# Two planes for the experts' rows and a fourth column sum held back, in a two-block fp32 kernel

## The chip, the cores and the metric

The kernel runs on one core of one Trainium2 chip. The metric is the device time of one execution in microseconds (us), the median of several runs; lower is better. The profile describes one execution, which has a time of its own.

## The reference, cut to what matters

T = 1024 tokens of width D = 1024 in fp32 pass through two blocks. The first has gated linear attention, pooling and a mixture of experts; the second a gated convolution and a dilated window attention.

```
h = rmsnorm(x, g1);  proj = h @ w_in          # q, k, v, r, a_low, u_pool, gates
log_a = log_sigmoid(a_low @ w_alpha_up + b) / 16
x = x + merged(gla, pool, gates) @ w_out
h2 = rmsnorm(x, g2)
# each token: the best of 4 groups, in it the 2 best of 8 experts (32 experts in all)
out[token] += gate * ((silu(h2 @ w_gate[e]) * (h2 @ w_up[e])) @ w_down[e])   # 2 rows a token
x = rmsnorm(x + out, gf)
# second block
proj2 = rmsnorm(x, norm_w) @ w_in_2           # conv part, q, k, v, z
for (window, dilation) in ((128,1), (512,4), (2048,16)):   # each of 8 heads
    banded softmax attention, with its log-sum-exp
y_attn = mix of the three by softmax of the log-sum-exps
x = x + concat(y_conv, y_attn * silu(z)) @ w_out_2
```

## The kernel before

All large products run in "split" fp32: an operand is written as a high part and a low part (ACT casts the high one, DVE subtracts the low one, both at L127), and `mm3` issues three matmuls (L161 to L163). A **column sum** (`cols_first`, L165) is 8 such triples, 24 matmuls of 512 columns, into one PSUM bank; `low_rank` (L177) is the like for the 16 low-rank columns of `a_low`. A framework inserts the waits: a tile is taken from a pool by tag, and an allocation waits until an older tile of that tag is free. The tag "blk" has 26 buffers of 4 KB a partition and serves almost every large tile; "wr" has 4 for raw weights, "vt" 3 for attention values. Order on each engine is program order. The program itself shifts steps: `late.at(n, fn)` runs `fn` n calls of `late.step()` later, and each column sum makes two such calls.

**Block 1** runs in two halves of 512 tokens (`half(0)`, `half(1)`). In half 0 the row scales of the first norm (1/rms) aren't ready when the first sums are. The low-rank sum and the sums of q0 and q1 are therefore held in PSUM without scales (`OWE = 3`). Then `h.owe` (L232) spreads the scales over partitions by 8 matmuls (L236) of the scales against an identity, and `take` (L245) multiplies the held sums while it copies them out. The steps are due at `2*OWE`, `2*OWE - 2 - 2*j` after their sums.

**Routing**: `route_rows(t)` takes each block of 128 tokens when its block-1 result x1 is finished. It writes x1 to `x_acc` in DRAM, turns it over on TensorE, computes logits, writes the scaled row h2 to `h2_d`. For the last block t = 7, h2 is made ahead of the logits by two POOL products (L531, L532). `slots` and `row_tables` produce, for each expert, the token numbers (`row_idx`) and weights (`row_wgt`) of up to 96 rows.

**Experts**: for each of 32 experts, POOL gathers 96 rows by an indirect DMA (L980), TensorE turns them, runs gate, up and down products with weights that SP loads in blocks of 512 KB, ACT scales the rows, and POOL adds them to `x_acc` by an indirect DMA that accumulates (`add_rows`, L985):

```
G.indirect_dma_start(out=x_acc, out_offset=..row_idx.., in_=src[:n], ..., compute_op=OP.add)
```

The rows of expert 31 stay on the chip and are added with selecting matmuls (`add_last`, L1068 to L1076). A loop for overflowing experts (L1128) runs zero times here. After it, `load_cols(x_acc, "x2c")` (L308) loads the first 512 tokens as four tiles of 256 columns; these loads wait for all the adds.

**Block 2** begins on those four tiles (second norm, turn, convolution products), then loads tokens 512 to 1023 (`load_x2`, L1219), then q, k, v. **Attention** is a stream of 48 items: 4 pairs of heads by 3 dilations by 4 parts. Per item: `load_values` (vt, SP), `powers` (scores at L1500, bias and minimum on DVE at L1506, exponential on ACT at L1508), `turn_powers` (transposes at L1526, copies at L1528 and L1530), `weigh` (L1559). The stream starts `powers` two items ahead of `weigh`. `by_class` (L1487) copies q and k into dilated order, on POOL, twice a pair of heads. `spread` (L1607) loads the mixing weights (zb), and `close_heads` (L1617) applies them. Between items stand pieces of the output product.

Of the kernel before, what the change touches and what calls it, by code (L numbers as in the profile page):

```python
# [20 lines left out]
P = 128  # L21
# [44 lines left out]
def first_then_second_block(ctx: ExitStack, tc: tile.TileContext, a: dict, out: bass.AP):  # L66
# [12 lines left out]
    OWE = 3  # L79
# [400 lines left out]
    row_idx = C.tile([P, NE], I32, name="row_idx")  # L480
    row_wgt = C.tile([P, NE], F32, name="row_wgt")
# [38 lines left out]
    last_h2 = []  # L520

    def route_rows(t, x1):
# [17 lines left out]
        def turn():  # L540
            for q in range(2):
                ps = psum((P, 4, P))
                for i in range(4):
                    PE.transpose(ps[:, i, :], xv[:, 4 * q + i, :], ident)
                split(hi[:, 4 * q:4 * q + 4, :], lo[:, 4 * q:4 * q + 4, :], ps)
            late.at(D2 if t < 4 else D5, logits)

# [12 lines left out]
        def folded(lt):  # L560
# [5 lines left out]
            if t < NT - 1:  # L566
                h2 = blk("h2", (P, D))
                V.scalar_tensor_tensor(h2, x1, r, g2, op0=OP.mult, op1=OP.mult)
                G.dma_start(h2_d[t * P:(t + 1) * P], h2)

# [17 lines left out]
    def route_half(hf):  # L588
# [26 lines left out]
        val = blk("val", (P, 4, 2, 5, NE), BF16)  # L615
        A.activation(val[:, :, :, 0, :], oh[:, ts], AF.Copy, scale=pcol)
        for i in range(4):
            A.activation(val[:, i, :, 1, :], oh[:, 4 * hf + i], AF.Copy, scale=float(4 * hf + i + 1))
        late.at(1 if hf else PLACES, lambda: places(hf, val, gp, e1, e2))

    def places(hf, val, gp, e1, e2):
# [31 lines left out]
        V.tensor_mul(val.rearrange("p t k v e -> p (t k) v e")[:, :, 2:, :],  # L653
# [4 lines left out]
    def slots(hf, val, sels):  # L658
        if hf == 0:
            slot_ps.append(psum((P, 5, NE)))  # L660
# [7 lines left out]
    def row_tables(idx, w, ps, n, pool):  # L668
        f = pool.tile([P, n], F32, name="ri_f", tag=f"rif{n}", bufs=1)
        e = pool.tile([P, n], F32, name="ri_e", tag=f"rie{n}", bufs=1)  # L670
        sv = pool.tile([P, 5, n], F32, name="ri_s", tag=f"ris{n}", bufs=1)
# [3 lines left out]
        V.scalar_tensor_tensor(idx, f, -float(P), e, op0=OP.add, op1=OP.add)  # L675
        V.tensor_add(e, sv[:, 2, :], sv[:, 3, :])
# [3 lines left out]
    def half(hf):  # L680
# [30 lines left out]
        else:  # L711
            w_q += pair(w_in, 0)
        if hf == 0:
# [21 lines left out]
        for j, w in enumerate(w_q):  # L735
            def emit_q(ps, j=j):
                if h.rb is None and hf == 0:
                    late.at(2 * OWE - 2 - 2 * j, lambda: h.take(qT[:, j, :], ps, 0.125))
                else:
                    h.take(qT[:, j, :], ps, 0.125)  # L740

            cols_first(w, h, emit_q)
        for j, w in enumerate(pair(w_in, 256)):
            cols_first(w, h, lambda ps: h.take(kT[:, j, :], ps))
# [223 lines left out]
    SY.dma_start(h2_d[(NT - 1) * P:], last_h2[0])  # L968
    load_expert(3)
    late.flush()  # L970
    row_tables(row_idx, row_wgt, slot_ps[0], NE, R)
# [63 lines left out]
    def down(e):  # L1035
# [10 lines left out]
        if e < NE - 1:  # L1046
            add_rows(yt, row_idx[:, e:e + 1], CAP)
# [9 lines left out]
    last_idx = S.tile([P, 1], I32, name="last_idx", bufs=1)  # L1057
    picks = blk("picks", (P, 512), F32R)

    def place_last():  # L1060
        at = S.tile([P, 5], F32, name="last_at", bufs=1)
        V.tensor_copy(last_idx, row_idx[:, NE - 1:NE])
        V.tensor_copy(at[:, 4:], last_idx)
        for i in range(4):
            V.tensor_scalar(at[:, i:i + 1], at[:, 4:], float(-P * i), None, op0=OP.add)
            V.tensor_scalar(picks[:, i * P:(i + 1) * P], iota_s, at[:, i:i + 1], None, op0=OP.is_equal)

    def add_last(c):  # L1068
        for j in range(2):
            ps = psum((P, 2, 256))  # L1070
            for i in range(2):
                b = 2 * j + i
                for part in range(2):
                    PE.matmul(ps[:, i, :], picks[:CAP, b * P:(b + 1) * P], last_y[1 + part][:CAP, 256 * c:256 * c + 256],
# [51 lines left out]

    end_reg = nc.values_load(n_more[0:1, 0:1], min_val=0, max_val=NOB)
    with tc.For_i(0, end_reg, 1):  # L1128
# [24 lines left out]
        rv = E.tile([P, NT, 2, 5], BF16, name="rv")  # L1153
# [5 lines left out]
        sp = psum((P, 5))  # L1159
# [7 lines left out]
        row_tables(li, lw, sp.rearrange("p (a b) -> p a b", b=1), 1, E)  # L1167
# [36 lines left out]
        add_rows(lyt, li, P)  # L1204
# [10 lines left out]
    def load_x2():  # L1215
        xs = []
        for t in range(4, NT):
            xt = blk(f"x2_{t}", (P, D))
            SY.dma_start(xt, x_acc[t * P:(t + 1) * P])  # L1219
            xs.append(xt)  # L1220
# [52 lines left out]
    yc = [blk("yc0", (P, T))] + [W.tile([P, T], F32, name=f"yc{j}") for j in range(1, 4)]  # L1273
# [3 lines left out]
    qT = [blk(f"qT{j}", (P, T)) for j in range(4)]  # L1277
    for j in range(4):
        V.memset(qT[j][:, 0:1], 0.0)
        V.memset(kT[j][:, 0:1], 0.0)  # L1280
# [5 lines left out]
    def conv(hf, cc):  # L1286
# [35 lines left out]
        def convolve(m):  # L1322
            ct, u = 2 * cc + m, us[m]
            cv = yc[ct]
# [85 lines left out]
    for f in c0[:4] + c1[:4] + c0[4:] + c1[4:] + attn_gate(0):  # L1410
        f()
    x2 = load_x2()
# [167 lines left out]
    def mix_weights(hp):  # L1580
# [16 lines left out]
        def spread():  # L1597
            ps = psum((48, P))
            PE.transpose(ps, sw.rearrange("p c h b -> p (c h b)"), ident)
            swT = W.tile([48, P], F32, name="swT", tag="swT", bufs=1)  # L1600
# [84 lines left out]
    for g in range(-2, NS):  # L1685
        if g + 2 < NS:
            hp, cfg, pr = stream[g + 2]
            if g == -2:
# [89 lines left out]
```

## Time and profile before

| | |
|---|---|
| median of 3 runs | 1626.17 us (1624.89 to 1628.64) |
| the profiled execution, its own time | 1627.21 us |
| its span | 1625.5 us |
| mean granted TensorE clock | 0.972 |
| DMA, mean over the span | 167 GB/s, 272.01 MB |

PE is TensorE's matmuls, DVE VectorE, ACT ScalarE, POOL GpSimd, SP the engine that issues most loads. The span runs from the first to the last instruction of the profiled execution; its time is a little longer. A granted clock of 1.00 is the full level, 0.50 half of it.

### The profile page before, as it was taken

Reading aid. Unit: us, or ns where it says so; the run is one execution under the profiler, and the core shown is the slowest. Engines: PE = TensorE matmul, PEld = TensorE weight load, DVE = VectorE, ACT = ScalarE, POOL = GpSimd, SP = SyncE. Lnnn points to the kernel's source line nnn. Section 1 sums busy time; section 2 is a strip of 40 time slices with the busy share of each in tenths; the row PEclk is TensorE's granted clock in tenths of the full one; section 3 lists DMA queues with packets and bytes.
Section 4 is the critical chain, followed back from the end, with each engine's and each line's share of the span. In section 5 each row is a group of like instructions: output and inputs, shape, how many; then the busy total and the mean of one; then the engine's idle time right before and its main releaser. Section 6 shows DMA issues by size and latency. Waiting matters only on the chain. (4 is left out here: it accounts for less than half of the span.)

```text
span 1625.5 us, 24026 instructions
## 1 busy us (share of the span) xinstructions
PE 1535.9 (94%) x8678; PEld 1266.6 (78%) x8678; DVE 1021.1 (63%) x2278; ACT 801.2 (49%) x1635; POOL 210.8 (13%) x196
## 2 busy tenths in 40 slices
PE   7999999999999994999989897999999999999899
PEld 6888888887888874998888786888877787666667
DVE  5596444667644355998877686766655545676663
ACT  4434323453433232888777684524443326866550
POOL 1000000000000003232232111200000100243311
PEclk9999999999999996999999998999999999999999
DMA  6233334436323458999999996434423331445445
GB/s 193 65 82 106 103 109 163 136 115 195 104 80 115 142 215 281 295 270 319 328 312 335 296 335 194 156 102 164 149 88 104 104 103 41 120 119 147 103 137 169
DMA packets 168022, 272.01 MB, mean 167 GB/s; under 512 B 32689, under 2 KB 111932, under 8 KB 167773
## 3 DMA queue, kind: packets, MB, share of 16 engines
q1 hardware_dynamic: 154204, 232.13, 44.5%
q0 software_dynamic: 13680, 38.32, 8.5%
q8 instruction: 69, 1.13, 0.3%
q14 instruction: 53, 0.43, 0.1%
q10 hardware_dynamic: 16, 0.00, 0.0%
HBM read 243.92 MB, written 39.59 MB: 174 GB/s over the span
## 5 line engine op out<-in xcount | busy, mean ns | idle before, releaser
L127 ACT CAST wh<-wr 128x512 fp32r<-128x512 f32 (+1 forms) x248 | 170.6, 716 | 341.9 <-PE ps L162 192.5
L127 DVE TENSOR_TENSOR wl<-wr,wh 128x512 fp32r<-128x512 f32 (+1 forms) x248 | 202.3, 832 | 169.4 <-ACT wh L127 162.7
L127 DVE TENSOR_TENSOR wl<-ew,wh 128x1024 fp32r<-128x1024 f32 x144 | 172.6, 1220 | 44.3 <-ACT wh L127 43.6
L161 PE MATMUL ps<-h,wh 128*128 128x512 f32 x448 | 176.8, 395 | 0.0
L127 ACT CAST wh<-ew 128x1024 fp32r<-128x1024 f32 x144 | 149.7, 1052 | 54.4 <-PE ps L163 34.8
L163 PE MATMUL ps<-h,wl 128*128 128x512 f32 x448 | 175.3, 391 | 0.0
L162 PE MATMUL ps<-h,wh 128*128 128x512 f32 x448 | 175.3, 391 | 0.0
L161 PE MATMUL ps<-g,wh 128*128 128x512 f32 x320 | 126.1, 395 | 0.0
L162 PE MATMUL ps<-g,wh 128*128 128x512 f32 x320 | 125.2, 392 | 0.0
L163 PE MATMUL ps<-g,wl 128*128 128x512 f32 x320 | 124.8, 391 | 0.0
L161 PE MATMUL ps<-wh,xh 128*96 128x256 f32 x384 | 112.3, 293 | 6.2 <-ACT act L1023 6.2
L162 PE MATMUL ps<-wl,xh 128*96 128x256 f32 x384 | 110.9, 289 | 1.5 <-DVE wl L127 1.5
L163 PE MATMUL ps<-wh,xh 128*96 128x256 f32 x384 | 110.8, 289 | 0.0
L163 PEld LDWEIGHTS ps<-h,wl 128*128 128x128 f32 x448 | 84.6, 189 | 17.8
L161 PEld LDWEIGHTS ps<-h,wh 128*128 128x128 f32 x448 | 84.7, 189 | 17.5
L162 PEld LDWEIGHTS ps<-h,wh 128*128 128x128 f32 x448 | 84.6, 189 | 17.2
L985 POOL DMA_INDIRECT x_acc<-yt,row_idx x31 | 52.1, 1679 | 208.2 <-ACT yt L1045 147.6
L161 PE MATMUL ps<-wh,g 128*128 128x512 f32 x192 | 76.3, 398 | 0.0
L528 POOL DMA_DIRECT2D x_acc<-x x7 | 3.8, 536 | 551.7 <-DVE x L930 294.0
L163 PE MATMUL ps<-wh,g 128*128 128x512 f32 x192 | 75.1, 391 | 0.0
L162 PE MATMUL ps<-wl,g 128*128 128x512 f32 x192 | 74.9, 390 | 0.0
L161 PEld LDWEIGHTS ps<-wh,xh 128*96 128x96 f32 x384 | 65.8, 171 | 8.2 <-ACT act L1023 7.0
(455 smaller groups left out, 3642.0 us busy)
## 6 DMA issues: line engine op xcount, KB each, us to landing
wr<-in_w_in_dram SPq DMA_DIRECT2D x128, 512.0 KB, 3.9
ew<-in_w_exp_down_dram SPq DMA_DIRECT2D x64, 512.0 KB, 9.7
ew<-in_w_exp_gate_dram SPq DMA_DIRECT2D x64, 512.0 KB, 8.0
ew<-in_w_exp_up_dram SPq DMA_DIRECT2D x64, 512.0 KB, 9.5
wr<-in_w_out_dram SPq DMA_DIRECT2D x24, 512.0 KB, 3.9
xs<-xb_rows POOLq DMA_DIRECT2D x28, 256.0 KB, 3.3
x<-in_x_dram SPq DMA_DIRECT2D x12, 512.0 KB, 6.3
zb<-sw_d SPq DMA_DIRECT2D x24, 256.0 KB, 5.2
```

Of the source, the lines that this page charges most:

```text
L127: both = A.copy(hi, src), V.tensor_sub(lo, src, hi.bitcast(F32))
L161: PE.matmul(ps, lhs[0], rhs[0], start=start, stop=False)
L162: PE.matmul(ps, lhs[0], rhs[1], start=False, stop=False)
L163: PE.matmul(ps, lhs[1], rhs[0], start=False, stop=stop)
L528: G.dma_start(x_acc[t * P:(t + 1) * P], x1)
L985: G.indirect_dma_start(out=x_acc, out_offset=bass.IndirectOffsetOnAxis(ap=idx[:n], axis=0), in_=src[:n], in_offset=None, bounds_check=T - ...
```

## The change

Five edits stand in one diff.

1. `OWE` 3 to 4: the column sum of k0 is also held without scales, so `h.owe` comes after it.
2. Experts' rows are written to rows of their own, in two planes of a DRAM array `y_d` of 2T rows (plane k for a token's k-th expert, `put_rows`), instead of added to `x_acc`. For that the slot product has a sixth column (k), `row_tables` makes `row_place`; 8 writes of 512 KB zeros clear rows 0 to 511 of both planes during half 1. The x2c loads are moved ahead of the overflow loop; after it 8 loads "y2c" bring the two planes, and `add_last` adds them (2 more DVE operations for each of 4 tiles). `load_x2` has 8 more loads and 8 more additions.
3. In `route_rows` the POOL products of the last block are gone: the block before waits with its h2 until the last block has been turned, and the last block's h2 is made on DVE after its logits; its write goes through POOL's queue in place of SP's.
4. `picks`, `yc[0]` and `qT` are allocated later.
5. Attention: `LEAD` 3 instead of 2, 4 "vt" buffers instead of 3, the copies of `by_class` on DVE, `swT` in tag "tmp".

```diff
-    OWE = 3
+    OWE = 4
...
+    y_d = tc.dram_tile([2 * T, D], F32, name="y_rows")
...
-        else:
-            h2 = blk("h2", (P, D))
-            G.tensor_mul(h2, x1, r.to_broadcast([P, D]))
-            G.tensor_mul(h2, h2, g2)
-            G.dma_start(x_acc[t * P:(t + 1) * P], x1)
-            last_h2.append(h2)
...
+            while unscaled:
+                unscaled.pop()()
...
+            if t == NT - 2 and NT - 1 not in turned:
+                unscaled.append(scaled_rows)
+            else:
+                scaled_rows()
...
-        val = blk("val", (P, 4, 2, 5, NE), BF16)
+        val = blk("val", (P, 4, 2, 6, NE), BF16)
...
+        for k in range(2):
+            A.activation(val[:, :, k, 5, :], oh[:, ts, k, :], AF.Copy, scale=float(k))
...
+        V.scalar_tensor_tensor(f, sv[:, 5, :], float(T), f, op0=OP.mult, op1=OP.add)
+        V.scalar_tensor_tensor(place, f, -float(P), e, op0=OP.add, op1=OP.add)
...
+        if hf == 1:
+            zero = blk("zero", (P, D))
+            G.memset(zero, 0.0)
+            for i in range(8):
+                r0_ = T * (i // 4) + P * (i % 4)
+                late.at(2 * i, lambda r0_=r0_: SY.dma_start(y_d[r0_:r0_ + P], zero))
...
-    def add_rows(src, idx, n):
-        G.indirect_dma_start(out=x_acc, out_offset=bass.IndirectOffsetOnAxis(ap=idx[:n], axis=0),
-                             in_=src[:n], in_offset=None, bounds_check=T - 1, oob_is_err=False, compute_op=OP.add)
+    def put_rows(src, place, n):
+        G.indirect_dma_start(out=y_d, out_offset=bass.IndirectOffsetOnAxis(ap=place[:n], axis=0),
+                             in_=src[:n], in_offset=None, bounds_check=2 * T - 1, oob_is_err=False)
...
     def add_last(c):
+        for y in yc2[c]:
+            V.tensor_add(xc2[c], xc2[c], y)
...
+    xc2, turn_part2 = load_cols(x_acc, "x2c")
     end_reg = nc.values_load(n_more[0:1, 0:1], min_val=0, max_val=NOB)
     with tc.For_i(0, end_reg, 1):
...
-    xc2, turn_part2 = load_cols(x_acc, "x2c")
-    add_rows(last_y[0], last_idx, CAP)
+    yc2 = []
+    for c in range(4):
+        yc2.append([])
+        for k in range(2):
+            yt = blk("y2c", (P, 4, 256))
+            SY.dma_start(yt, y_d[T * k:T * k + 512, 256 * c:256 * c + 256].rearrange("(i p) n -> p i n", p=P))
+            yc2[c].append(yt)
+    put_rows(last_y[0], last_place, CAP)
...
             SY.dma_start(xt, x_acc[t * P:(t + 1) * P])
+            for k in range(2):
+                yt = blk("y2", (P, D))
+                SY.dma_start(yt, y_d[T * k + t * P:T * k + (t + 1) * P])
+                V.tensor_add(xt, xt, yt)
...
-        v = hd[hp]["v"][cfg, pr] = W.tile([P, 3, P], F32, name="vt", tag="vt", bufs=3)
+        v = hd[hp]["v"][cfg, pr] = W.tile([P, 3, P], F32, name="vt", tag="vt", bufs=4)
...
-            G.tensor_copy(dst, src.rearrange("p (l r) -> p r l", r=n))
+            V.tensor_copy(dst, src.rearrange("p (l r) -> p r l", r=n))
...
-    for g in range(-2, NS):
+    LEAD = 3
+    for g in range(-LEAD, NS):
```

## Rows read from the trace of the kernel before

**Rows 1.** The page's busy time of each engine, share, instructions.
```profile
PE 1535.9 (94%) x8678; PEld 1266.6 (78%) x8678; DVE 1021.1 (63%) x2278; ACT 801.2 (49%) x1635; POOL 210.8 (13%) x196
```
**Rows 2.** Windows by stage: length, busy PE PEld DVE ACT POOL, granted clock, DMA share, GB/s.
```profile
0.00:60.00 60.00, 51.07 (x228) 41.16 (x229) 31.45 (x79) 30.20 (x66) 7.97 (x25) 0.94 0.52 157
60.00:580.00 520.00, 520.00 (x2555) 427.54 (x2554) 301.26 (x664) 194.49 (x342) 4.28 (x8) 1.00 0.39 121
...
764.00:976.00 212.00, 189.51 (x1291) 169.60 (x1290) 159.09 (x193) 157.29 (x224) 48.35 (x33) 0.94 0.97 321
976.00:1016.00 40.00, 30.20 (x155) 24.62 (x154) 24.18 (x38) 18.37 (x38) 4.87 (x4) 0.83 0.70 194
1016.00:1356.00 340.00, 335.99 (x1529) 276.31 (x1528) 204.05 (x483) 131.52 (x258) 27.44 (x27) 1.00 0.37 118
1356.00:1572.00 216.00, 198.85 (x1563) 142.79 (x1562) 135.41 (x523) 146.40 (x531) 57.46 (x45) 0.96 0.44 118
```
**Rows 3.** Timeline around the row scales: start, us, engine, line, idle before and releaser.
```profile
27.09 0.39 PE L163 MATMUL ps<-h,wl 128*128 128x512 f32 x1
...
28.55 1.22 DVE L127 TENSOR_TENSOR wl<-wr,wh 128x1024 fp32r<-128x1024 f32 x1
...
30.96 2.05 PE L236 MATMUL ps<-ident,rsq_y 128*128 128x128 f32 x8 [3.49 <-DVE rsq_y L106]
...
32.66 0.77 PE L161 MATMUL ps<-h,wh 128*128 128x512 f32 x1
...
36.57 0.39 PE L161 MATMUL ps<-h,wh 128*128 128x512 f32 x1
```
**Rows 4.** Timeline of POOL in the routing, 585 to 668.
```profile
618.16 2.77 POOL L531 TENSOR_TENSOR h<-x,rsq_y 128x1024 f32<-128x1024 f32 x1 [2.89 <-DVE rsq_y L106]
621.01 2.35 POOL L532 TENSOR_TENSOR h<-h,g 128x1024 f32<-128x1024 f32 x1
```
**Rows 5.** Windows: an add beside weight loads, an add alone, loads alone.
```profile
840.00:844.00 4.00, 3.60 (x31) 3.53 (x31) 4.00 (x5) 3.95 (x7) 2.59 (x2) 1.00 1.00 381
...
987.30:992.50 5.20, 0.00 (x0) 0.00 (x0) 0.69 (x1) 1.16 (x2) 1.38 (x1) 0.97 0.39 60
995.00:997.00 2.00, 1.00 (x5) 0.71 (x4) 0.10 (x1) 0.00 (x0) 0.00 (x0) 0.50 1.03 347
```
**Rows 6.** Timeline between the experts and block 2.
```profile
986.80 0.40 PE L163 MATMUL ps<-wh,ah 128*96 128x512 f32 x1
...
987.26 1.42 POOL L985 DMA_INDIRECT x_acc<-yt,row_idx  x1 [4.58 <-ACT yt L1045]
...
993.31 2.02 SPq L308 DMA_DIRECT2D x2c<-x_acc  x4
...
996.90 1.28 DVE L1076 TENSOR_TENSOR x2c<-x2c,ps 128x512 f32<-128x512 f32 x2 [2.10 <-DMA x2c<-x_acc]
```
**Rows 7.** Timeline of SP around the second half's loads, 1095 to 1165.
```profile
1110.35 2.04 SPq L1219 DMA_DIRECT2D x<-x_acc  x4
1115.37 38.63 SPq L116 DMA_DIRECT2D wr<-in_w_in_dram  x8
```
**Rows 8.** Lines of DVE by shape, whole span: times, busy, mean ns, idle before.
```profile
L1238 DVE TENSOR_TENSOR u<-x,gf 128x1024 f32<-128x1024 f32 x4 | 4.8, 1219 | 0.5 <-ACT sq L1239 0.5
...
L1245 DVE TENSOR_SCALAR u<-u,rsq_y 128x1024 f32<-128x1024 f32 x4 | 2.8, 744 | 0.0
```
**Rows 9.** Timeline of all engines in the attention, 1498 to 1513.
```profile
1503.78 2.08 POOL L1487 COPY qd<-qT 128x1024 f32<-128x1024 f32 x1
1503.96 4.95 DVE L127 TENSOR_TENSOR wl<-wr,wh 128x1024 fp32r<-128x1024 f32 x1
...
1508.84 0.41 DVE L1506 CUSTOM_DVE_ANT_0 sb<-ps,b 128x256 f32<-128x256 f32 x1
```
**Rows 10.** Timeline of SP in the attention, 1355 to 1570.
```profile
1470.11 3.65 SPq L1607 DMA_DIRECT2D zb<-sw_d  x6
...
1475.19 0.57 SPq L1464 DMA_DIRECT2D vt<-v_rows  x1
```
**Rows 11.** Waits in the attention, 1356 to 1572: us in total, times, longest.
```profile
PE ps L1526 <- ACT sb L1508: 9.1, 8, 2.7
...
PE ps L1559 <- DMA vt<-v_rows: 6.3, 3, 2.7
```

More of the change, by code (lines that the diff above doesn't have):

```diff
@@ L517, in first_then_second_block @@
     lgs = {}
-    last_h2 = []
+    turned, unscaled = set(), []
     def route_rows(t, x1):
@@ L666, in slots, with row_tables @@
                           start=t == 0 and k == 0, stop=t == NT - 1 and k == 1)
-    def row_tables(idx, w, ps, n, pool):
+    def row_tables(idx, place, w, ps, n, pool):
         f = pool.tile([P, n], F32, name="ri_f", tag=f"rif{n}", bufs=1)
         e = pool.tile([P, n], F32, name="ri_e", tag=f"rie{n}", bufs=1)
-        sv = pool.tile([P, 5, n], F32, name="ri_s", tag=f"ris{n}", bufs=1)
+        sv = pool.tile([P, 6, n], F32, name="ri_s", tag=f"ris{n}", bufs=1)
         V.tensor_copy(sv, ps)
@@ L734, in half, with emit_qk @@
         qT, kT = blk("qT"), blk("kT")
-        for j, w in enumerate(w_q):
-            def emit_q(ps, j=j):
+        for j in range(4):
+            def emit_qk(ps, j=j):
+                dst, scale = (qT[:, j, :], 0.125) if j < 2 else (kT[:, j - 2, :], 1.0)
                 if h.rb is None and hf == 0:
-                    late.at(2 * OWE - 2 - 2 * j, lambda: h.take(qT[:, j, :], ps, 0.125))
+                    late.at(2 * OWE - 2 - 2 * j, lambda: h.take(dst, ps, scale))
                 else:
[L740 to L744, printed above, removed]
+                    h.take(dst, ps, scale)
+            if j == 2:
+                w_q += pair(w_in, 256)
+            cols_first(w_q[j], h, emit_qk)
         vN = [blk(f"v{j}") for j in range(2)]
@@ L1073, in add_last @@
                 for part in range(2):
-                    PE.matmul(ps[:, i, :], picks[:CAP, b * P:(b + 1) * P], last_y[1 + part][:CAP, 256 * c:256 * c + 256],
+                    PE.matmul(ps[:, i, :], picks[0][:CAP, b * P:(b + 1) * P], last_y[1 + part][:CAP, 256 * c:256 * c + 256],
                               start=part == 0, stop=part == 1)
@@ L1219, in load_x2 @@
             SY.dma_start(xt, x_acc[t * P:(t + 1) * P])
+            for k in range(2):
+                yt = blk("y2", (P, D))
+                SY.dma_start(yt, y_d[T * k + t * P:T * k + (t + 1) * P])
+                V.tensor_add(xt, xt, yt)
             xs.append(xt)
@@ L1272, in first_then_second_block @@
     w_in2 = a["w_in_2"]
-    yc = [blk("yc0", (P, T))] + [W.tile([P, T], F32, name=f"yc{j}") for j in range(1, 4)]
+    yc = [None] + [W.tile([P, T], F32, name=f"yc{j}") for j in range(1, 4)]
     edge = W.tile([P, 4, 2], F32, name="edge")
@@ L1276, in first_then_second_block @@
     kT = [B.tile([P, T], F32, name=f"kT{j}", tag="wb", bufs=4) for j in range(4)]
[L1277 to L1280, printed above, removed]
     v_d = tc.dram_tile([T, 512], F32, name="v_rows")
@@ L1323, in convolve @@
             ct, u = 2 * cc + m, us[m]
+            if yc[ct] is None:
+                yc[ct] = blk("yc0", (P, T))
             cv = yc[ct]
@@ L1411, in first_then_second_block @@
         f()
+    qT = [blk(f"qT{j}", (P, T)) for j in range(4)]
+    for j in range(4):
+        V.memset(qT[j][:, 0:1], 0.0)
+        V.memset(kT[j][:, 0:1], 0.0)
     x2 = load_x2()
@@ L1599, in spread @@
             PE.transpose(ps, sw.rearrange("p c h b -> p (c h b)"), ident)
-            swT = W.tile([48, P], F32, name="swT", tag="swT", bufs=1)
+            swT = W.tile([P, 512], F32, name="swT", tag="tmp", bufs=NTMP)[:48, :P]
             A.copy(swT, ps)
@@ L1684, in first_then_second_block @@
     NS = len(stream)
-    for g in range(-2, NS):
-        if g + 2 < NS:
-            hp, cfg, pr = stream[g + 2]
-            if g == -2:
+    LEAD = 3
+    for g in range(-LEAD, NS):
+        if g + LEAD < NS:
+            hp, cfg, pr = stream[g + LEAD]
+            if g == -LEAD:
                 begin_heads(hp)
```

38 lines of the change are left out of this document (22 added, 16 removed).

## The prediction

> **What bounds the kernel now.** I read first the busy time per engine: matmuls run 94% of the span [rows 1], so only the time in which TensorE stands still, or runs at a lower clock, can be won. The windows by stage show where that is [rows 2]. From 60 to 580 and from 1016 to 1356 PE is busy for 520.0 of 520 and 336.0 of 340 us: nothing done beside it there can help. It stands still for 8.9 us at the start, 22.5 among the late experts, 9.8 between the experts and block 2, and 17.2 in the attention; the granted clock of those stretches is 0.94, 0.94, 0.83 and 0.96. Each stage has its own limit, so I then went stage by stage through timelines, waits and DMA rates. The late experts run with the DMA engines 97% busy [rows 2]; the gap behind them is a wait for an accumulating write; the attention waits for chains of small operations.
>
> **The change part by part.** Terms are made against the profiled execution's own 1627.21 us (span 1625.5), which is 1.04 above the median 1626.17; 1.0 is taken off at the end.
>
> *Four sums held.* PE ends the third sum at 27.48 and idles 3.49 us for the scales; then 8 spreading matmuls stand from 30.96 to 32.66 and 9 matmuls of the next sum from 32.66 to 36.57, both at half clock (0.77 us for a matmul that takes 0.39 at 36.57) [rows 3]. With a fourth sum ahead, 24 matmuls at about 0.23 us or 5.4 us run in that gap, past the moment when the scales are ready (30.8). Won: 3.49, half of the 3.91 us of the nine (1.95) and half of the 1.70 of the eight (0.85), together 6.3. The fourth sum needs k0's weights: DVE's split stands at 28.55 to 29.77, so in the worst case PE starts it 2 us late; that and the one more held copy make the ends -4.5 and -6.3. I take **-6.3**, because the DVE work ahead of 28.55 is already most of these weights.
>
> *Routing.* POOL's two products, 2.77 and 2.35 us [rows 4], go; DVE gets one product of the last block after its logits, about 1.2 to 1.3 us (an estimate from a DVE product of this size, 1.22 us [rows 8]). The sixth slot column adds two small activations per half and the tables two DVE operations over 32 columns, a few tenths of a us each. The write of the last rows now goes in POOL's queue ahead of the first gather. PE is stalled in this stretch, so all of it counts: the last rows come about 2 us earlier, the longer tables give back some 1.3. **-0.7**, with ends -1.3 and +1.3.
>
> *Zeros.* 8 writes of 512 KB in half 1, where the DMA share is 0.39 [rows 2], and one memset on a POOL that is busy 4.28 us in 520. The low DMA share hides them; without that cover they would take about 8 times 1.5 us (512 KB at 347 GB/s [rows 5]). **0**, ends 0 and +2.
>
> *Experts: plain writes in place of additions.* An addition alone moves 60 GB/s over 5.2 us, 0.31 MB, and keeps the DMA engines busy for 0.39 of that, 2.03 us. Loads alone move 347 GB/s at a share of 1.03 over 2 us, so 0.31 MB of loads would use 0.9 us [rows 5]. The excess is 1.1 us an expert, and 19 experts lie in the stretch from 764 to 976, which is at 97%: 21 us. Against this stands the window with an addition in flight and loads around it: 381 GB/s at a share of 1.00 [rows 5], no worse than loads alone, so most of the excess may overlap. No row shows a plain indirect write. The ends are -21 and 0. Two thirds I give to the overlap, since the 381 is the nearer row, and take **-7**. The 22.5 us that PE idles here, and 0.06 of 212 us in the clock [rows 2], leave room for it.
>
> *Between the experts and block 2.* Before, the last expert matmul stands at 986.80, the last addition is issued at 987.26, and the x2c loads start only at 993.31; the first tile is summed at 996.90 [rows 6]. After, x2c is loaded ahead, and the wait is for a plain write to y_d, which I estimate 2 to 3 us shorter than the 5.2 of the addition (0.31 MB at load rate is 0.9 us, behind the 1.42 us of issue). But instead of four loads of 512 KB there are eight, 12 us in place of 6 at 1.5 us each, and DVE has 8 more additions of 1.22 us (two inputs in SBUF, [rows 8]), 9.8 us. The first pair arrives about 4 us earlier and the fourth some 2 later, so PE starts sooner and goes more slowly. **0**, ends -4 and +6.
>
> *Second half of x2.* SP's four loads at 1110.35 become twelve, and behind them in SP's queue stand the next 8 weight loads at 1115.37 [rows 7]; 8 more loads are 12 us of transfers at a DMA share of 0.37 [rows 2]. The 8 additions are 9.8 us of DVE, which works 204 of 340 us here. Both are covered unless the weights behind them become late: they are just in time already (the eight are issued over 38.6 us, each when a buffer is free [rows 7]). 8 loads of 1.5 us, less the 5 us between 1110.35 and 1115.37 in which SP waits, could cost 7; most of it TensorE's queued work absorbs. **+2.5**, ends 0 and +6.
>
> *Attention.* A DVE subtraction of two SBUF operands took 4.95 us beside two POOL copies of 2.08 and 2.02 us, where its kind takes 1.23 to 1.29; the scores behind it on DVE started only at 1508.84 [rows 9]. So a POOL copy sits in the way of DVE, and DVE in the way of PE. The copies now stand on DVE: 16 of 128x1024, strided, so between 0.74 us (one contiguous SBUF input), 1.22 (two) [rows 8] and POOL's own 2.1: 12 to 34 us, taken as 19.5 (the 1.22, since the stride costs something). DVE idles 80.6 of 216 us here, which hides them on the whole; two in a row cost the scores behind them at most 2.4 us where that cover is gone. LEAD 3 gives each item one more stage of slack, and with the fourth vt buffer a load no longer waits for the item just ahead. PE's waits named here are 9.1 us for the exponential and 6.3 for vt [rows 11], of 17.2 idle and 0.04 of 216 us (8.6) in the clock [rows 2]: 25.8 in all. The row nearest to what the edit does is the sum of the two waits, 15.4, halved because other chains (the output weights, the mixing weights) end close behind: **-8**, ends 0 and -17 (all the idle time).
>
> By the Trainium skill ("SBUF — State Buffer", Who interferes with whom) a DVE operation with two SBUF inputs and a GpSimd operation that reads SBUF lock each other out for the whole instruction; the 4.95 us agree. By that rule each of the 16 copies removed could give back its 2.1 us to DVE, 33 us against the 19.5 added, and the term would come near -15 instead of -8, the sum to about -26.5. I keep the row's.
>
> **Sum**: -6.3 - 0.7 + 0 - 7 + 0 + 2.5 - 8 = -19.5; 1627.2 - 19.5 - 1.0 = 1606.7, so **1607**.
>
> **The rivals.**
>
> *Relief that doesn't reach PE.* The additions overlap fully, the expert stage stays bound by the bytes of its weights (97% DMA share [rows 2]), and the attention waits move to the next chain. For it: 381 GB/s with an addition in flight. Against it: the 4.95 us row and the two named waits. Terms -6.3 - 0.7 + 2.5 = -4.5: 1621.7.
>
> *Additions at their price alone.* The full 21 us come back, and the attention gives 14 (nearly all of the 15.4). For it: 97% share, where any DMA time should count. Against it: the 381 again, and that PE's own work between the stalls bounds the gain at the 22.5 us and the clock. Transition and second half at 0: -6.3 - 0.7 - 21 - 14 = -42: 1584.
>
> *Slower: the 26 "blk" buffers run out in the attention.* LEAD 3 keeps one more item's scores, its copies and its next pair's qd and kd alive, and the three zb tiles are taken at the same moment: by my count of allocations and last uses about 27 buffers are wanted at a change of heads, 23 to 24 before. Then SP waits for a zb buffer, and behind its zb loads stands the next vt load, as it stands 5.1 us behind it now (1470.11, 1475.19 [rows 10]). That would be about 7.5 us at each of 4 changes, +30 instead of -8: 1645. It decides from 3.7 us a change on (the other terms are -11.5, and 3.25 must be passed: 14.75 / 4). Against it: the waits of before show no buffer of this tag, and q is freed as pairs of heads end. The Trainium skill ("Perfetto Trace Analysis", Optimization Strategy) says that gaps which repeat can mean that no room is left for the next tile; no such row is in the trace of before, and it would give the same +30.
>
> **How the numbers follow.** A change below 0.2%, 3.25 us, can't be told from none. Forecast 0.62, no relief 0.18, full price 0.11, slower 0.09. The forecast's own range is 1594 (experts and attention -14 each, as a half-way to their ends) to 1618 (-3 each, and +2 between the stages). The range 1590 to 1623 adds the case of no relief and leaves out the last two, 0.20. Of the 0.18, 0.08 falls within 0.2% (1623 and up to 1629, when the second half costs its +6); the rest is faster. Faster 0.62 + 0.11 + 0.10 = 0.83, same 0.08, slower 0.09.
>
> **What would show it.** In the profile after: no idle time before L236 and a granted clock near 1.00 from 27 to 37; PE's period per expert between 764 and 976 shorter at the same GB/s or higher; the put landing in under 5 us, first y2c sums by about 993 and TensorE's up-product no earlier than before; the third weights of the second half later by up to 3 us with PE idle there; L1526's wait for the exponential and L1559's for vt together under 8 us, POOL without copies. A vt or zb load on SP that waits for a buffer at each change of heads would show the slower rival. The prediction is wrong if the expert stage keeps its length and the attention too, or if the additions on DVE between the stages end on PE's path by their full 9.8 us.

## The result, and the profile after

The changed kernel takes 1590.68 us (median of 4, 1589.86 to 1590.89) against 1626.02 before (4 runs): the ratio is 0.9779, interval 0.9763 to 0.9796, 35 us faster. The forecast was 1607 with a range from 1590 to 1623; the time lies 0.7 us inside its lower end. The profiled execution took 1589.86 us, its span is 1588.1, its mean granted clock 0.982 (0.972 before).

Where the 37.4 us of span went is read from the first and last start of certain matmuls, in the view of one source line. Of the kernel before (L1031 turns an expert's activations, L229 the x2c tiles, L1500 scores, L1559 weighs the values):

```profile
L1031 PE MATMUL ps<-ident,act x64: 247/282/284, 655.6 to 982.9; 96*128 96x96 f32 x64
...
L229 PE MATMUL ps<-ident,x2c x32: 271/370/477, 997.6 to 1012.8; 128*128 128x128 f32 x32
...
L1500 PE MATMUL ps<-kd,qd x256: 271/322/428, 1353.2 to 1543.6; 64*128 64x192 f32 x64, 64*128 64x128 f32 x64
...
L1559 PE MATMUL ps<-pt,vt x640: 268/273/477, 1368.5 to 1564.7; 128*64 128x128 f32 x120, 64*64 64x128 f32 x40
```

Of the changed kernel, the same places:

```profile
L1048 PE MATMUL ps<-ident,act x64: 246/283/284, 649.0 to 960.2; 96*128 96x96 f32 x64
...
L229 PE MATMUL ps<-ident,x2c x32: 270/273/477, 977.2 to 995.7; 128*128 128x128 f32 x32
...
L1536 PE MATMUL ps<-kd,qd x256: 272/322/427, 1336.6 to 1500.2; 64*128 64x192 f32 x64, 64*128 64x128 f32 x64
...
L1595 PE MATMUL ps<-pt,vt x640: 269/273/462, 1358.4 to 1527.4; 128*64 128x128 f32 x120, 64*64 64x128 f32 x40
```

Differences of neighbouring times make a table of stages; the start ends at the first turn of the linear attention's output (134.2 before, 127.6 after). Every run of the study is in it, by its profiled execution, so that one can see both an edit's effect and how far a stage that it doesn't touch moves by itself (experts with plain writes 305 to 317, attention with LEAD 3 and copies on VectorE 188 to 194). A row shows one execution; the ratio in the last column is that of the medians.

| kernel | start | to the experts | experts | to x2c's last turn | to the scores | attention | rest | ratio to before (interval) |
|---|---|---|---|---|---|---|---|---|
| before | 134.2 | 521.4 | 327.3 | 29.9 | 340.4 | 211.5 | 60.8 | |
| changed | 127.6 | 521.4 | 311.2 | 35.5 | 340.9 | 190.8 | 60.7 | 0.978 (0.976 to 0.980) |
| its term | -6.6 | 0.0 | -16.1 | +5.6 | +0.5 | -20.7 | -0.1 | |
| forecast | -6.3 | -0.7 | -7 | 0 | +2.5 | -8 | 0 | |
| three sums | 133.6 | 523.7 | 312.1 | 35.9 | 340.8 | 193.7 | 60.7 | 0.983 (0.979 to 0.986) |
| accumulating, two planes | 126.8 | 523.2 | 328.9 | 39.7 | 340.5 | 189.3 | 60.7 | 0.992 (0.989 to 0.995) |
| before, plain writes | 133.5 | 521.6 | 309.7 | 27.1 | 340.6 | 213.8 | 60.8 | 0.985 (0.981 to 0.988) |
| LEAD 2 | 128.1 | 524.4 | 309.4 | 35.1 | 340.9 | 207.7 | 60.9 | 0.992 (0.989 to 0.995) |
| copies on GpSimd | 128.3 | 522.8 | 311.1 | 36.0 | 340.8 | 206.3 | 60.7 | 0.986 (0.982 to 0.991) |
| before, copies on VectorE | 134.5 | 523.3 | 324.1 | 30.5 | 340.6 | 206.6 | 60.8 | 0.996 (0.994 to 0.997) |
| LEAD 2, heads not closed | 126.1 | 521.7 | 310.6 | 35.5 | 340.6 | 203.8 | 60.9 | 0.984 (0.981 to 0.988) |
| LEAD 4 | 127.8 | 523.1 | 313.3 | 35.9 | 340.9 | 200.4 | 59.2 | 0.984 (0.981 to 0.987) |
| no plane additions | 127.1 | 522.8 | 306.7 | 34.3 | 340.6 | 188.4 | 60.7 | 0.975 (0.972 to 0.979) |
| expert 30 held | 127.3 | 523.9 | 311.5 | 34.3 | 340.5 | 192.8 | 60.7 | 0.977 (0.973 to 0.981) |
| held, two tiles early | 128.4 | 524.2 | 316.7 | 36.1 | 340.5 | 192.2 | 60.9 | 0.981 (0.979 to 0.983) |
| last rows early | 128.4 | 521.1 | 305.2 | 34.8 | 340.9 | 189.9 | 60.7 | 0.977 (0.974 to 0.979) |

Windows of the changed kernel, to be read against [rows 2] (length, busy PE, PEld, DVE, ACT, POOL, clock, DMA share, GB/s): the start, the experts, the stretch behind them in two halves, the attention. Below them stands the attention of the kernel before, cut at the same matmuls.

```profile
0.00:60.00 60.00, 54.06 (x257) 43.95 (x258) 35.38 (x95) 33.62 (x75) 7.98 (x25) 1.00 0.53 157
...
649.00:960.20 311.20, 296.20 (x2141) 268.64 (x2141) 265.46 (x336) 258.49 (x367) 70.70 (x56) 0.98 0.95 327
...
970.00:985.00 15.00, 7.80 (x35) 6.71 (x35) 10.35 (x12) 2.29 (x4) 0.00 (x0) 0.61 0.94 313
985.00:1000.00 15.00, 13.43 (x67) 10.74 (x67) 13.06 (x18) 6.99 (x22) 0.91 (x1) 0.92 0.81 247
...
1336.60:1527.70 191.10, 185.74 (x1557) 137.88 (x1556) 133.30 (x533) 142.71 (x525) 30.79 (x33) 0.99 0.48 130
```
```profile
1353.20:1565.00 211.80, 195.67 (x1557) 141.05 (x1556) 132.52 (x519) 143.60 (x524) 57.46 (x45) 0.96 0.44 117
```

In the start the clock is 1.00 where it was 0.94, with 3 us less idle time. In the attention PE idles 5.4 us instead of 16.1, and the same 1557 matmuls are busy 185.7 us instead of 195.7: half of the gain is idle time, half is matmuls that take less time. Of the second half the clock explains about 7 us (an estimate: 0.04 of 211.8 us against 0.01 of 191.1); where the other 3 come from isn't shown.

### The profile page after: what moved, and what is told of

Same layout as the page of the kernel before. It is cut to its first block, busy times and chain, and to the rows that moved or that the text cites. A ratio compares the mean times of both kernels' runs of the same rounds, so it can differ in the third digit from the quotient of the medians.

```text
span 1588.1 us, 24023 instructions
## 1 busy us (share of the span) xinstructions
PE 1512.4 (95%) x8678; PEld 1253.1 (79%) x8678; DVE 1042.5 (66%) x2313; ACT 801.8 (50%) x1639; POOL 160.0 (10%) x180
## 5 line engine op out<-in xcount | busy, mean ns | idle before, releaser
L127 DVE TENSOR_TENSOR wl<-wr,wh 128x512 fp32r<-128x512 f32 (+1 forms) x248 | 195.8, 807 | 156.4 <-ACT wh L127 152.7
L161 PE MATMUL ps<-wh,xh 128*96 128x256 f32 x384 | 110.3, 287 | 6.0 <-ACT act L1040 6.0
L163 PE MATMUL ps<-wh,xh 128*96 128x256 f32 x384 | 109.1, 284 | 0.0
L163 PEld LDWEIGHTS ps<-h,wl 128*128 128x128 f32 x448 | 84.1, 188 | 17.7
L161 PEld LDWEIGHTS ps<-h,wh 128*128 128x128 f32 x448 | 84.1, 188 | 17.7
L161 PEld LDWEIGHTS ps<-g,wh 128*128 128x128 f32 x320 | 60.2, 188 | 13.0 <-issue 0.6
L162 PEld LDWEIGHTS ps<-g,wh 128*128 128x128 f32 x320 | 60.4, 189 | 12.7 <-DVE g L130 0.5
L163 PEld LDWEIGHTS ps<-g,wl 128*128 128x128 f32 x320 | 60.4, 189 | 12.4
```

The source lines that it names most:

```text
L127: both = A.copy(hi, src), V.tensor_sub(lo, src, hi.bitcast(F32))
L161: PE.matmul(ps, lhs[0], rhs[0], start=start, stop=False)
L162: PE.matmul(ps, lhs[0], rhs[1], start=False, stop=False)
L163: PE.matmul(ps, lhs[1], rhs[0], start=False, stop=stop)
```

## The experiments

**The fourth sum.** `OWE = 4` back to `3`:

```diff
-    OWE = 4
+    OWE = 3
```

> The changed kernel with three sums held instead of four. Theory: the 3.5 us wait for the row scales and the half clock behind it come back, every later stage 6.5 us later, 1597. Rival (the shift is taken up at the experts, whose weights set their pace): 0 to 2 us slower, 1592.

Measured: 1600.09 us, ratio 0.983. The start is 6.0 us longer and TensorE's wait for the scales is back (4.52 us), as the theory has it; the rest of the difference in this profile (experts +0.9, routing +2.3, attention +2.9) is within what these stages do by themselves. The rival, that the experts take the shift up, falls. In the changed kernel the spreading matmuls follow the fourth sum without a wait:

```profile
32.36 1.05 PE L236 MATMUL ps<-ident,rsq_y 128*128 128x128 f32 x8
```

**Accumulating writes, from both sides.** In the changed kernel the put accumulates (into cleared rows of its own, for which 8 more zero writes stand in half 1); in the kernel before the addition becomes a plain write, so that its sums are lost:

```diff
-                             in_=src[:n], in_offset=None, bounds_check=2 * T - 1, oob_is_err=False)
+                             in_=src[:n], in_offset=None, bounds_check=2 * T - 1, oob_is_err=False, compute_op=OP.add)
```

> The changed kernel with accumulating writes of the experts' rows, each still to its own row of the two planes; all rows of the planes are cleared first, 8 more writes of 512 KB in half 1. The stretch from the first to the last turn of an expert's activations took 327 us before and 311 after. Theory (the accumulation costs DMA time in a stretch bound by it): 327 us again, 310 GB/s in it, the kernel 17 us slower, 1608. Rival (the gain came from the writes no longer waiting for one another's rows, or from the earlier start): at most 4 us slower, 1595.

```diff
-                             in_=src[:n], in_offset=None, bounds_check=T - 1, oob_is_err=False, compute_op=OP.add)
+                             in_=src[:n], in_offset=None, bounds_check=T - 1, oob_is_err=False)
```

> The kernel before with plain indirect writes to x_acc in place of the accumulating ones, so that a token's row holds what was written last and not the sum. Theory (the accumulation's DMA time): 16 us faster over the experts and 1 us at the end of them, 1609. Rival (order among the writes or the start): at most 4 us faster, 1622.

Measured: 1612.70 us with accumulating planes, 1606.01 for the kernel before with plain writes. The windows of the expert stage: accumulating planes, then the kernel before, then the kernel before with plain writes.

```profile
650.00:979.00 329.00, 305.11 (x2142) 275.09 (x2141) 265.86 (x336) 257.43 (x366) 84.85 (x56) 0.96 0.95 308
```
```profile
655.60:982.90 327.30, 304.53 (x2141) 274.12 (x2140) 265.27 (x336) 257.58 (x367) 82.03 (x56) 0.96 0.95 309
```
```profile
655.10:965.00 309.90, 298.02 (x2142) 269.88 (x2141) 265.94 (x337) 258.53 (x367) 72.45 (x56) 0.97 0.94 326
```

The stage moved by +17.7 and by -17.6 us, one attribute each way, with the DMA engines at a share of 0.94 to 0.95 in all: with accumulation they move 308 GB/s in it, without 326. The engines are as full; what fills them is worth less. 17.6 us over 31 writes is 0.57 us of DMA time each, half of the excess of 1.1 us that an addition alone shows [rows 5]. Each of these differences is between two executions of a stage that moves by some us; over all kernels of the table the three with accumulation take 326.8 us in the mean and the eleven with plain writes 310.7, which is 0.52 us a write, and the two groups don't overlap. The planes themselves, order and earlier start explain none of it beyond that scatter. The write's landing also counts once at the end: the stretch to x2c's last turn is 4.2 us longer with accumulation in the changed kernel and 2.8 shorter without it in the one before.

Where the saved time appears can be read from the gathers, one per expert. Before, they come 9.5 us apart in the mean up to 760.77, and the next 12.5 us later. In the changed kernel they come 9.6 us apart up to 811.94, and the next 16.2 us later. These next ones:

```profile
773.28 1.01 POOL L980 DMA_INDIRECT xg<-h_rows,row_idx  x1 [0.30 <-issue]
```
```profile
828.13 1.52 POOL L997 DMA_INDIRECT xg<-h_rows,row_idx  x1 [9.15 <-PE ps L1048]
```

The early experts are no faster; their cheaper writes let TensorE run on for six experts more before the pace breaks.

**Attention: slack or copies.** Three kernels: LEAD 2 in the changed one, the copies on GpSimd in the changed one, the copies on VectorE in the kernel before.

```diff
-    LEAD = 3
+    LEAD = 2
```

> The changed kernel with LEAD back at 2 (four vt buffers and the copies on VectorE stay). The attention, from the first scores to the last weighing, took 211.8 us before and 191.1 after. Theory (the gain is the third stage of slack): about 205 us there, the kernel 14 us slower than the changed one, 1605. Rival (the gain is that the copies left GpSimd): 196 us there, 5 us slower, 1596.

```diff
-            V.tensor_copy(dst, src.rearrange("p (l r) -> p r l", r=n))
+            G.tensor_copy(dst, src.rearrange("p (l r) -> p r l", r=n))
```

> The changed kernel with the 16 copies of q and k back on GpSimd (LEAD 3 stays). Theory (slack is most of the attention's gain): 6 us slower than the changed kernel, 1597, since three stages cover most of a VectorE operation held up by a copy. Rival (the copies are most of it): 14 us slower, 1605, with VectorE operations of 3 to 5 us beside the copies again.

```diff
-            G.tensor_copy(dst, src.rearrange("p (l r) -> p r l", r=n))
+            V.tensor_copy(dst, src.rearrange("p (l r) -> p r l", r=n))
```

> The kernel before with its 16 copies of q and k on VectorE and nothing else changed (LEAD 2, three vt buffers). Theory (slack is most of the attention's gain): 5 us faster than before, 1621. Rival (the copies are most of it): 14 us faster, 1612. A third possibility, that copies on VectorE cost without the third stage: slower by 3, 1629.

Measured: 1612.58, 1604.74 and 1622.69 us. The first run alone would read as if slack were most of the gain (its theory's side), the second as if the copies were (its rival's side), the third as if they were little (its theory's number). Together they say that neither edit is the gain by itself. Taking back LEAD costs 16.9 us of attention, taking back the copies 15.5; but either edit alone is worth only some 5 (copies alone 211.5 to 206.6, LEAD with GpSimd copies 206.3), and both 20.7. Some ten of the 20.7 us come only when both are there, more than the 5 us by which the attention moves by itself. LEAD 3 here always has the fourth vt buffer; with LEAD 2 that buffer shows no gain (206.6 us without, 207.7 with it), and LEAD 3 without it wasn't tried. Waits of PE in the attention: LEAD 2, then copies on GpSimd, then the changed kernel (before: [rows 11]).

```profile
PE ps L1562 <- ACT sb L1544: 11.5, 7, 3.3
```
```profile
PE ps L1595 <- ACT pt L1564: 8.2, 4, 4.2
PE ps L1562 <- DVE xs L1692: 2.6, 2, 2.3
PE ps L1595 <- DVE tok L1542: 1.7, 2, 0.8
```
```profile
PE ps L1595 <- ACT pt L1564: 4.2, 2, 2.8
PE ps L1595 <- DVE pt L1566: 1.1, 3, 0.4
```

With LEAD 2 the old wait of the transposes for the exponentials stays (9.1 before, 11.5 here). With LEAD 3 and copies on GpSimd it is gone, and a new one stands in its place: the weighing waits for PSUM copies. The timeline of that kernel at the first change of heads shows what delays VectorE and with it the scores:

```profile
1416.42 4.03 DVE L1653 TENSOR_TENSOR og<-og,zb 128x512 f32<-128x512 f32 x2
...
1417.44 2.46 POOL L1523 COPY qd<-qT 128x1024 f32<-128x1024 f32 x1
...
1419.85 2.51 POOL L1523 COPY kd<-kT 128x1024 f32<-128x1024 f32 x1
...
1420.38 3.13 DVE L1655 TENSOR_TENSOR og<-og 128x512 f32<-128x512 f32 x2
...
1424.77 0.66 PE L1562 MATMUL ps<-ident,sb 128*128 128x128 f32 x4 [2.34 <-DVE xs L1692]
```

The copies come late, queued on GpSimd behind the closing products, which wait for zb. Beside them two VectorE products take 4.03 us and two sums 3.13; in the changed kernel each of these operations takes 0.69. By the Trainium skill ("SBUF — State Buffer", Who interferes with whom) operations with two SBUF inputs and GpSimd operations that read SBUF exclude each other for a whole instruction; these rows agree.

These closing products on VectorE are also what the kernels with one edit undone have in common. In the attention they take 0.69 us each with both edits, 1.50 with LEAD 2 (beside GpSimd's own closing products and sums, at the first change of heads from 1411.46 to 1420.76), 1.56 with the copies on GpSimd, 1.34 with the copies alone and 1.30 before. The changed kernel, then LEAD 2:

```profile
L1653 DVE TENSOR_TENSOR og<-og,zb 128x512 f32<-128x512 f32 x6 | 3.9, 685 | 0.0
```
```profile
L1653 DVE TENSOR_TENSOR og<-og,zb 128x512 f32<-128x512 f32 x6 | 8.8, 1504 | 0.0
```

That this is why the two edits need each other is not shown: it goes with the gain, but LEAD 4 has it too (0.68 us) with an attention of 200.4 us, and no run changes it alone.

**What LEAD 2 lacks.** I then took the closing block for the thing that two items can't outlast, since at 1424.50 of the LEAD 2 run PE idles 3.12 us behind 7 us of it on VectorE:

```profile
1424.50 1.10 PE L1562 MATMUL ps<-ident,sb 128*128 128x128 f32 x3 [3.12 <-ACT sb L1544]
```

The products and sums of `close_heads` were left out, with LEAD 2:

```diff
-    LEAD = 3
+    LEAD = 2
...
-        for b in range(2):
-            sl = halves[b]
...
-            V.tensor_mul(y, y, za[b][hp // 2][:, hp % 2, :])
         ys.append(og[0])
```

> The changed kernel with LEAD at 2 and without the products and sums that apply the mixing weights when a pair of heads is closed (VectorE and GpSimd; the attention output is the first dilation's alone). LEAD 2 made the attention 207.7 us long instead of 190.8, with TensorE's waits at the changes of heads behind 7 us of these operations on VectorE. Theory (two stages of slack are too few for exactly that block): the waits at the changes vanish and the attention takes 188 to 193 us. Rival (two stages are too few everywhere): 202 us or more.

Measured: 1602.23 us. The attention took 203.8 us: 4 us for the block, and the rival is right. The waits behind the block are gone, but TensorE's waits for the exponentials still come to 11.8 us (11.5 with the block): 10.0 of them now stand at two places where another operation is in front of the exponentials, a cast of an output weight on ScalarE that waits for its load. The first of the two:

```profile
1475.06 1.04 ACT L127 CAST wh<-wr 128x1024 fp32r<-128x1024 f32 x1 [6.82 <-DMA wr<-in_w_out_dram]
1476.01 0.50 ACT L1544 ACTIVATE sb<-sb,tok 128x256 f32<-128x256 f32 x1
...
1476.66 0.69 PE L1562 MATMUL ps<-ident,sb 128*128 128x128 f32 x2 [3.57 <-ACT sb L1544]
```

With a third item in flight neither wait is in the changed kernel's list. More isn't better:

```diff
-    LEAD = 3
+    LEAD = 4
...
-            load_values(hp, cfg, pr)
             powers(hp, cfg, pr)
...
+        if 0 <= g + 3 < NS:
+            load_values(*stream[g + 3])
```

> The changed kernel with LEAD 4 (values still loaded three items ahead, four vt buffers). In the changed kernel's attention TensorE idles 5.4 of 191.1 us at a clock of 0.99; with LEAD 2 it idled 12.5 at 0.96. Theory (operations that stand ahead of the scores on ScalarE and VectorE, such as a cast that waits for an output weight, are outlasted by more items in flight): 187 us for the attention, the kernel 3 us faster than the changed one. Rival (buffers and the order on VectorE are used up; a fourth stage holds more tiles without use): 191 us or more, the kernel the same or up to 10 us slower.

Measured: 1601.52 us, with 200.4 us in the attention, the rival's side. PE's waits in it:

```profile
PE ps L1595 <- ACT pt L1564: 8.7, 10, 2.4
PE ps L1595 <- DVE pt L1566: 1.3, 3, 0.5
```

The weighing now waits for the PSUM copies on ScalarE ten times instead of twice. That exponentials of items further ahead stand in front of these copies would explain it; it wasn't tried by itself.

**Between the experts and block 2.** First the 8 additions away, then expert 30's rows held on the chip, so that the plane loads needn't wait for their write:

```diff
-        for y in yc2[c]:
-            V.tensor_add(xc2[c], xc2[c], y)
```

> The changed kernel without the 8 additions of the planes to the x2c tiles (the loads stay; the experts' rows are missing for tokens 0 to 511). The stage between the experts and block 2 became 5.6 us longer with the change. Theory (the loads of the planes set its pace: VectorE waited for them before most additions): 2 us faster than the changed kernel, 1589. Rival (the additions' 9.8 us on VectorE are the path): 6 to 9 us faster, 1583.

```diff
-        if e < NE - 1:
+        if e < NE - HELD:
             put_rows(yt, row_place[:, e:e + 1], CAP)
...
+    HELD = 2
...
+                for m in range(HELD):
                     for part in range(2):
...
-    put_rows(last_y[0], last_place, CAP)
+    for m in range(HELD):
+        put_rows(last_y[m][0], last_place[:, m:m + 1], CAP)
```

> The changed kernel, with the rows of expert 30 held on the chip like those of expert 31 and added by selecting matmuls (32 more of 256 columns), and written to the planes at the end. The plane loads wait for the write of expert 30, which is issued 965.34 and landed at 970.1. Theory (the wait for the last write and the loads behind it are the path): loads start at about 962, first sum 8 us earlier, less 3 us for the matmuls, 5 us faster, 1586. Rival (VectorE's additions or the extra matmuls and splits are the path): no faster or up to 3 us slower, 1591 to 1594.

Without the additions the stretch is 34.3 us instead of 35.5 (34.8 to 36.0 in the kernels that leave it alone): 1.2 us gained and not 9.8 (the faster total, 1588.18, rests on stages that the edit doesn't touch). That is the theory's number, but the edit takes away the theory's wait as well: without the additions no instruction waits for the planes. The first turn of x2c comes 12.4 us after the last turn of an expert's activations instead of 17.0, and the last one hardly earlier, because TensorE then stands still for block 2's first weights. Timeline of that kernel:

```profile
983.77 0.62 ACT L127 CAST wh<-wr 128x512 fp32r<-128x512 f32 x1 [7.84 <-DMA wr<-in_w_in_dram]
...
986.54 0.80 PE L161 MATMUL ps<-g,wh 128*128 128x512 f32 x1 [6.18 <-ACT g L129]
```

This cast comes 27.2 us after the experts here, 27.9 in the changed kernel (at 988.12, behind a wait of 2.71 for the load) and 22.2 in the kernel before; in all kernels of the table but one (two tiles early) the last turn follows it by 6.2 to 8.2 us, whether the stretch is 27.1 us long or 39.7. So the weights behind the 8 plane loads set the end of the stretch. That goes by these times; no run moves the weights alone. The changed kernel's timeline:

```profile
965.34 1.41 POOL L1002 DMA_INDIRECT y_rows<-yt,row_place  x1 [7.63 <-ACT yhl L127]
...
970.10 7.69 SPq L1235 DMA_DIRECT2D y2c<-y_rows  x8
970.61 2.08 PE L1094 MATMUL ps<-yhl,picks 96*128 96x256 f32 x8 [6.07 <-issue]
973.69 1.23 DVE L1088 TENSOR_TENSOR x2c<-x2c,y2c 128x1024 f32<-128x1024 f32 x1 [6.50 <-DMA y2c<-y_rows]
975.17 1.23 DVE L1088 TENSOR_TENSOR x2c<-x2c,y2c 128x1024 f32<-128x1024 f32 x1 [0.26 <-DMA y2c<-y_rows]
```

The first loaded tile is used at 973.69, against 996.90 before [rows 6], 23.2 us earlier while the experts ended 22.7 earlier: nothing is won there. Behind the first load VectorE hardly waits for the others (0.26 us at 975.17), and block 2's weights, issued from 979.63, queue behind the 8 loads at a DMA share of 0.94. Holding expert 30 didn't start the loads sooner (971.80); it took 1592.25 us, the rival's number. In that kernel PE waits 4.0 us for the overflow loop, which runs zero times and still lets no engine through before VectorE's last split at 970.7. So the loads of two tiles were moved ahead of the loop:

```diff
     xc2, turn_part2 = load_cols(x_acc, "x2c")
+    yc2 = [[blk("y2c", (P, 4, 256)) for k in range(2)] for c in range(2)]
+    load_planes(range(2))
...
         put_rows(lyt, lp, P)
+        load_planes(range(2))
```

> The changed kernel with expert 30 held on the chip as in the run before, and the plane loads of the first two column tiles moved ahead of the overflow loop (repeated in its body). With expert 30 held alone, those loads started at 971.8, not at 962: the loop makes every engine wait for the last split on VectorE (970.7). Theory (the loop is the gate): these four loads start before 966, VectorE's first addition at about 971 instead of 976.3, and from the last turn of an expert's activations to the last turn of x2c it takes 31 us, not 35.5; 4 us faster than the changed kernel, 1588. Rival (whatever comes first, the second two tiles and the weights behind them set the pace): 35 us, 1592.

36.1 us, the rival's number, but not for its reason; the total, 1598.70, is slower than both forecasts, with 5.5 us more in the experts, for which no cause is known. Timeline of SP in that kernel:

```profile
966.55 6.21 SPq L1157 DMA_DIRECT2D y2c<-y_rows  x4
972.86 2.82 SPq L116 DMA_DIRECT2D wr<-in_w_in_dram  x2
984.86 2.02 SPq L1157 DMA_DIRECT2D y2c<-y_rows  x4
```

SP's order put block 2's weight loads ahead of the loop too; one waited 12.7 us for a buffer, and PE stood 8.0 us at the loop for SP. Whether plane loads ahead of the loop would help with those weights behind it stays open.

**The last rows of the routing.** With the change the last slot product starts at 624.6 instead of 633.1, the first gather at 631.24 instead of 635.18: 8.5 us earlier, then only 3.9. Timeline of the changed kernel:

```profile
623.34 1.28 DVE L567 SCALAR_TENSOR_TENSOR h<-x,rsq_y,g 128x1024 f32<-128x1024 f32 x1
...
624.91 0.53 POOL L568 DMA_DIRECT2D h_rows<-h  x1 [9.81 <-DVE h L567]
...
625.36 1.97 DVE L681 TENSOR_SCALAR ri_e<-ri_s 128x32 f32<-128x32 f32 x1
...
627.37 0.19 DVE L683 SCALAR_TENSOR_TENSOR row_idx<-ri_f,ri_e 128x32 int32<-128x32 f32 x1
...
631.24 1.05 POOL L997 DMA_INDIRECT xg<-h_rows,row_idx  x1 [3.96 <-issue]
```

The row numbers are ready at 627.6, the gather starts 3.7 us later, 6.3 after the row write was issued. To take that write off the path, the product was written ahead of the choice of experts:

```diff
             V.tensor_copy(lt, ps)
+            if t == NT - 1:
+                scaled_rows()
             late.at(D3 if t < 4 else D6, lambda: folded(lt))
```

> The changed kernel with the last block's scaled rows computed right behind its logits' copy, ahead of the choice of experts, instead of behind the slot products on VectorE. With the change the first gather came 6.6 us after the last slot product, 2.1 before it. Theory (the gather waits until that row write has landed): about 3 us after the slot product, slot products at most 1 us later, expert stage 2 us earlier, 1590. Rival (the longer tables or the filling of tiles on GpSimd set it): 6 to 7 us again, and 1 us slower, 1593.

Inconclusive: VectorE ran the product at 623.30 and the write was issued at 624.87, as before the edit, and the gather came at 631.55. In the order that ran, the product still stands behind the whole choice of experts, ahead only of one product (L663 at 624.49) that the slots need, so the statement ahead of the prediction that each engine follows the program's order is too simple. That the gather waits for that write is supported by the transfers that the traces recorded, though no run takes the write away: in nine kernels the last packet of this 512 KB write ends 1.3 to 1.6 us before the gather starts, while the gather comes 3.6 to 5.7 us after the row numbers are ready. The difference to the changed kernel, 0.977 to 0.978, is none.

## Why the prediction came out as it did

The direction was right and the range held the time, by 0.7 us. The sum, -19.5, was half of the span's -37.4, and the time lies nearer to the second rival (1584) than to the forecast: the two large terms were mis-sized. That the range held the time is in part luck: the experts and the attention together gave 21.8 us more than forecast, and 5.6 us between the stages were lost against them.

1. The fourth sum: -6.3 forecast, -6.6 measured, 6.0 by undoing it. The idle time before the spreading matmuls is gone and they take 1.05 us instead of 2.05.
2. Routing: -0.7 forecast, 0.0 measured, within its ends. The chain up to the slots became 1.9 us shorter (497.0 us from the first turn of the linear attention's output, 498.9 before), as forecast, and the way from there to the first expert as much longer: the price that the sum gave to the longer tables is, by the times above, that of the late row write.
3. Zeros: 0, right; no stage shows them.
4. Experts: -7 forecast, -16.1 measured, 17.6 and 17.7 by the two experiments. The mechanism was right, the size wrong by two steps of the sum. It counted only the 19 additions between 764 and 976, where PE waits; but weights are loaded ahead, so the stretch up to 764, in which PE never waits (108.00 of 108 us busy from 656), passes its DMA time on (the gathers run on to 811.94), and all 31 count. And it gave two thirds of the excess to overlap because one window with an addition in flight moved 381 GB/s; measured over the stage and 31 writes, half is paid (0.52 to 0.57 of 1.1 us).
5. Between the experts and block 2: 0 forecast, +5.6 measured, inside the end of +6. I took the shorter landing for a gain of 4 us at the first pair; the first tile came no earlier against the experts' end. The longer transfers that I did count delayed something that I left out here, block 2's first weights: their cast comes 5.7 us later against the experts' end. The additions aren't on the path by their full 9.8 us, the sign of being wrong that the prediction named.
6. Second half: +2.5 forecast, +0.5 measured. Twelve loads and 8 additions are covered by work.
7. Attention: -8 forecast with an end at -17, -20.7 measured, outside. The step that failed is halving the two waits of 15.4 us because other chains end close behind, with nothing added for the clock. Those chains were there (the casts of output weights, the closing block), but with both edits neither holds TensorE: both waits are gone whole, new ones come to 5.3 us, and the idle time fell by 10.7 us. The rest of the 20.7, 9.9 us, is matmuls that take less time, some 7 of it the clock, which the prediction had priced at 8.6 us and left out of the term. The copies on VectorE take 1.15 us each, near the 1.22 of the sum. The estimate by the rule of the Trainium skill ("SBUF — State Buffer", Who interferes with whom), -15 (33 less the 19.5 gives 13.5), was nearer, yet the copies by themselves give 4.9: the price is that of the pair of edits.

Of the rivals, relief that doesn't reach PE is refuted by both experiments on the writes. The slower one didn't occur with LEAD 3: no wait of TensorE repeats at each change of heads, and no row names a wait for a zb buffer. The Trainium skill ("Perfetto Trace Analysis", Optimization Strategy) says that repeated gaps can mean missing room; the gaps that repeat in the kernels with one edit undone are named in the rows by operations queued ahead on ScalarE, VectorE and GpSimd instead.

No variant of the study beats the changed kernel by more than the intervals allow.

## What to carry to other kernels

In a stage bound by transfers, price every transfer of the stage, also those issued while the compute engine is still busy: prefetching hands their time on. Two edits on one chain of small operations can be worth little apart and much together, so the waits that each would leave behind have to be priced jointly, with the clock that idle time costs. An order written in the source isn't the order that runs; read it from the trace before costing a moved step.

## What the runs showed of the hardware

The granted clock fell to its half level behind a short wait. In the attention of the kernel before, TensorE was busy for 2.42 of 4.5 us at 0.98, the end of which was a wait of 2.12 us up to 1439.54; in the next 3.5 us the granted clock was 0.50.

```profile
1435.00:1439.50 4.50, 2.42 (x26) 1.56 (x22) 4.50 (x12) 1.51 (x5) 1.31 (x2) 0.98 0.36 113
1439.50:1443.00 3.50, 3.46 (x14) 1.95 (x16) 2.09 (x12) 3.36 (x16) 1.33 (x2) 0.50 0.46 121
1443.00:1447.00 4.00, 4.00 (x24) 2.89 (x24) 1.83 (x9) 2.05 (x8) 3.22 (x2) 0.61 0.48 113
```

A VectorE operation over 32 columns with one SBUF input (L681, 625.36) took 1.97 us beside a fill of two tiles on GpSimd; where the fill was over, in the kernel with the last rows early, it took 0.18.

```profile
625.43 1.86 POOL L994 MEMSET xg<- 128x1024 f32 x2
```
```profile
627.39 0.18 DVE L683 TENSOR_SCALAR ri_e<-ri_s 128x32 f32<-128x32 f32 x1
```
